# A two-layer gated encoder in one core: later stores of keys and values, gate products copied out of their banks, an earlier attention, and last tiles in halves

## The chip, the cores and the metric

The kernel runs on one core of one Trainium2 chip. The time is device time in microseconds (us). The kernel before takes 2231.48 us, the median of 3 runs (2231.09 to 2231.74). A profile and a trace of one execution stand beside it.

## The reference, cut to what matters

A trunk of 2 layers is applied to a prompt of 512 tokens and a sample of 1024 tokens, width 1024, all in float32:

```python
hn = rmsnorm(h, ln1[i]);  z = hn @ w_in[i]
q, k, v, ga, uf, gf, mga, mgf = split(z)
a = band_attention(rope(q), rope(k), v, sink[i]) * silu(ga)
f = fourier_mix(uf, w_fmix[i]) * silu(gf)
merged = sigmoid(mga) * (a @ w_ao[i]) + sigmoid(mgf) * (f @ w_fo[i])
h = h + merged @ w_out[i]
gate = sigmoid(rmsnorm(h, ln_pg[i]) @ w_pg[i])
h = h + (p[i] @ w_pe[i]) * gate
# after both layers
y = rmsnorm(h, ln_f)
```

## The kernel before, in words

**Tiles.** Tokens are cut into three chunks of 512 (`NCH`): chunk 0 is the prompt, chunks 1 and 2 the sample. Activations lie transposed, 128 channels by 512 tokens a tile. Every float32 product is made of three float32r matmuls of 512 columns (high by high, high by low, low by high; `mm3_steps`, L94), so that one output tile of 128 x 512 over 1024 channels is 24 matmuls. `hi_lo` (L84) makes the two halves: ScalarE casts (L86) and VectorE subtracts (L87).

**Stages of a layer.** `project_prompt` (L489) makes the 34 column tiles of `z` for chunk 0, in the order K, V, four of Q, then gates and U. `project_pair` (L503) makes them for chunks 1 and 2 together, two column tiles a round, by a Strassen-like scheme of 7 products (`Pair.steps`, L218) in three PSUM banks; a round has 14 steps of 6 matmuls, and its weights, 1 MB, are loaded by `Pair.load` (L192, DMAs of L195 and L196) from the third product of the round before. VectorE adds the banks up (L240 to L258). `merge` (L528) does the output projections and the gate, for chunk 0 alone (`mm_ps`, three banks of the tag mm) and then for chunks 1 and 2; in the last layer the gate of chunks 1 and 2 goes group by group, (1,) and then (2,).

**Who runs beside whom.** `run` (L938) steps a main generator (TensorE's stream of matmuls) and, from a given step on and at a given rate, a second one beside it. Beside `project_pair` runs the attention of the sample (`attention`, L668, slim: scores of a unit, loads of the next, four empty steps, values), from step 70, at 1.4 steps a step (L1036). A unit is one block of 128 queries and one key head.

**Late actions and the order of the queue.** `after(n, fn)` puts an action `n` ticks behind; `tick` runs what is due, once a step. `store` (L276) issues a DMA on SyncE's queue that way and pins it behind what stands on that queue already (`keep_in_program_order`). The queue issues in order: an issue that waits for its data holds up the loads behind it. K's stores are put 6 ticks behind, V's 3 (L440, L423). The order of everything that isn't pinned is a planner's, which sorts the instructions of each engine by program order and by when it expects their inputs. Tiles come from pools (45 tiles of 4 KB a partition under the tag act, 16 of 2 KB under scr) and are waited for when a pool is empty.

**The gate.** In `merge` the last product of a tile stays in its PSUM bank until `finish` (L580) has multiplied it (L585) by the row scale of the norm. For the first tile that scale is still to come: `norm2.stats` (L321: TensorE sums squares, L324; 12 small VectorE instructions) and `scale` (L338: four transposes, L341, and a copy, L343) come one tick behind. `finish` then does tanh on ScalarE (L586), two VectorE instructions (L587, L589), a square (L318) and its addition (L319).

**The end.** After chunk 1's and chunk 2's last tile `norm.stats` comes 1 tick and `result` (L594) 4 ticks behind: the scale, then eight tiles of the output, six by VectorE (L602) and two by ScalarE and GpSimd (L599, L600), each stored by one DMA (L603). For chunk 2 all of this comes after TensorE's last product.

Of the kernel before, what the change touches and what calls it, by code (L numbers as in the profile page):

```python
# [18 lines left out]
P = 128  # L19
# [3 lines left out]
T = 512  # L23
# [3 lines left out]
NCH = 3  # L27
EPS = 1e-6
# [11 lines left out]
def trunk(ctx: ExitStack, tc: tile.TileContext, x, p, w_in, w_af, w_out, w_pe, w_pg, w_fm,  # L40
# [53 lines left out]
    def mm3_steps(out, ws, xs, each):  # L94

        n = len(ws)
        for i, ((wh, wl), (xh, xl)) in enumerate(zip(ws, xs)):
            PE.matmul(out, wh, xh, start=i == 0, stop=False)  # L98
            PE.matmul(out, wh, xl, start=False, stop=False)  # L99
            PE.matmul(out, wl, xh, start=False, stop=i == n - 1)  # L100
            if (i + 1) % each == 0 and i + 1 < n:
                yield
# [205 lines left out]
    class Norm:  # L308
# [12 lines left out]
        def stats(self):  # L321
            st = pst("misc")
            for j in range(4):
                PE.matmul(st[:, j : j + 1], self.acc[:, j * P : (j + 1) * P], mean_sb, start=True, stop=True)  # L324

            v, y, z = (st[:, 4 * j : 4 * j + 4] for j in range(1, 4))
            r = sbt([P, 4], F32, "tiny")
            V.tensor_scalar(v, st[:, 0:4], EPS, None, op0=ALU.add)

            V.tensor_scalar(y.bitcast(I32), v.bitcast(I32), 1, None, op0=ALU.arith_shift_right)  # L330
            V.tensor_scalar(r.bitcast(I32), y.bitcast(I32), -1.0, float(0x5F3759DF), op0=ALU.mult, op1=ALU.add)
            for _ in range(3):
                V.tensor_tensor(z, v, r, op=ALU.mult)
                V.scalar_tensor_tensor(z, z, -0.5, r, op0=ALU.mult, op1=ALU.mult)
                V.scalar_tensor_tensor(r, z, 1.5, r, op0=ALU.add, op1=ALU.mult)
            self.r = r

        def scale(self):  # L338
            rb_ps, r = pst("misc"), self.r
            for j in range(4):  # L340
                PE.transpose(rb_ps[:, j * P : (j + 1) * P], r[:, j : j + 1].to_broadcast([P, P]), ident_sb)  # L341
            rb = scr()
            V.tensor_copy(rb, rb_ps)  # L343
            return rb
# [48 lines left out]
    class Projection:  # L393
# [19 lines left out]
        def transposed(self, a, c):  # L413
            s, pos = CHUNK_SEQ[c], CHUNK_POS[c]
            tp = pst("misc")
            for j in range(4):
# [7 lines left out]
                  f(t).rearrange("p j h d -> p j (h d)"), 3)  # L424

        def finish(self, m, c, out, in_sbuf):
# [9 lines left out]
            if m == MT_K:  # L436
                t = self.roped(out, c, 0)
                for r in (0, 64):
                    for kv in range(2):
                        store(K[s][r : r + 64, kv, :, pos : pos + T], f(t)[64 * kv : 64 * kv + 64], 6)  # L440
# [87 lines left out]
    def merge(l, chunks, parts, ws, bank, groups):  # L528
# [51 lines left out]
        def finish(m, c, out):  # L580
            if m == 0:
                rb[c] = norm2[c].scale()
            pl, a = scr(), scr()
# [10 lines left out]
        def result(c):  # L594
            r = norm[c].scale()
            for m in range(KD):
                o, h, g = scr(), hs[c][m // 2][:, m % 2, :], ln_sb[:, 4, m : m + 1]
                if m % 3 == 2:
                    S.activation(h, h, AF.Copy, scale=g)  # L599
                    G.tensor_tensor(o, h, r, op=ALU.mult)  # L600
                else:
                    V.scalar_tensor_tensor(o, h, g, r, op0=ALU.mult, op1=ALU.mult)  # L602
                SY.dma_start(y[c, m], o)  # L603

        for group in groups:
            for m in range(KD):
                w = ws.get()
                for c in group:
# [59 lines left out]
    def attention(l, chunks, slim):  # L668
# [91 lines left out]
        if slim:  # L760
            for u in range(len(units)):
# [3 lines left out]
                for _ in range(4):  # L765
# [243 lines left out]
    for l in range(DEPTH):  # L1009
# [21 lines left out]
        for _ in pair_made(xs, l, range(3, 4)):  # L1031
# [4 lines left out]
            (chain(attention(l, PAIR, True), mixed(0, range(8), fx)), 14 * 5, 1.4),  # L1036
# [120 lines left out]
```

## Time and profile before

| what | value |
|---|---|
| median of 3 runs | 2231.48 us |
| the profiled execution's own time | 2233.25 us |
| its span in the trace | 2231.5 us |
| TensorE busy | 2172.4 us, 97% of the span |
| VectorE, ScalarE, GpSimd busy | 1500.9, 1087.7, 297.3 us |
| TensorE's granted clock, mean | 0.991 of full speed |

A matmul's busy time is modelled and overlaps the next one's, so the list of waits (who waited for whom, and how long) says more than the busy share: TensorE's waits are where its stream broke. A wait is named by the engine and line that waited and by what came last before it went on.

### The profile page before, as it was taken

The page shows a single profiled execution, that of the slowest core. Times are in us where ns is not written, and L with a number is a line of the kernel's source. Part 1 is how long each engine was busy: PE and PEld are TensorE (multiplying, and loading weights), DVE is VectorE, ACT ScalarE, POOL GpSimd, SP SyncE. Part 2 cuts the span into 40 slices and gives each one's busy share as a digit, 9 for nine tenths or more (in the row PEclk, how much of TensorE's full clock was granted, in tenths as well). Part 3 has the DMA queues.
Part 4 walks back from the last instruction along what each step waited for, and adds up shares of the span by engine and source line. Part 5 has one row for each costly group of instructions (what it writes and reads, how often), then busy time and mean ns, then how long its engine had stood idle before and what let it go on. Part 6 is the DMA issues. An engine that isn't in the chain of part 4 may idle for free. (4 is left out here: it accounts for less than half of the span.)

```text
span 2231.5 us, 29985 instructions
## 1 busy us (share of the span) xinstructions
PE 2172.4 (97%) x10176; PEld 1803.0 (81%) x10176; DVE 1500.9 (67%) x2871; ACT 1087.7 (49%) x2324; POOL 297.3 (13%) x215
## 2 busy tenths in 40 slices
PE   9999999999999999999999999999999999999996
PEld 7778877788888878888888877778888888888885
DVE  5866576676678873464566766756766787854476
ACT  5576433566665454124324944236666644512342
POOL 0201110000002111222300010100000011231141
PEclk9999999999999999999999999999999999999998
DMA  8656454544448575532455555443444674653232
GB/s 305 221 175 210 159 173 149 159 133 153 137 153 294 190 259 190 202 104 71 144 180 170 166 171 189 160 151 128 154 152 143 208 260 170 218 203 118 78 126 99
DMA packets 241145, 380.69 MB, mean 171 GB/s; under 512 B 21216, under 2 KB 95584, under 8 KB 240992
## 3 DMA queue, kind: packets, MB, share of 16 engines
q1 hardware_dynamic: 234080, 366.19, 48.6%
q10 hardware_dynamic: 6912, 12.59, 1.5%
q8 instruction: 80, 1.31, 0.2%
q14 instruction: 73, 0.60, 0.1%
HBM read 270.17 MB, written 108.53 MB: 170 GB/s over the span
## 5 line engine op out<-in xcount | busy, mean ns | idle before, releaser
L229 PE MATMUL mm<-act,act 128*128 128x512 f32 x2856 | 694.4, 393 | 11.8 <-DVE scr L246 6.5
L229 PEld LDWEIGHTS mm<-act,act 128*128 128x128 f32 x2856 | 530.9, 188 | 124.1 <-ACT act L86 9.1
L98 PE MATMUL mm<-act,act 128*128 128x512 f32 x1384 | 545.9, 395 | 3.6 <-DVE scr L585 3.3
L100 PE MATMUL mm<-act,act 128*128 128x512 f32 x1384 | 544.2, 394 | 2.9 <-DVE act L87 2.8
L99 PE MATMUL mm<-act,act 128*128 128x512 f32 x1384 | 543.4, 393 | 0.0
L86 ACT CAST act<-act 128x512 fp32r<-128x512 f32 x574 | 329.2, 618 | 210.3 <-DMA act<-in_w_af 59.3
L87 DVE TENSOR_TENSOR act<-act,act 128x512 fp32r<-128x512 f32 x474 | 332.1, 735 | 32.4 <-ACT act L86 30.8
L100 PEld LDWEIGHTS mm<-act,act 128*128 128x128 f32 x1384 | 261.5, 189 | 59.9 <-DVE act L87 6.4
L98 PEld LDWEIGHTS mm<-act,act 128*128 128x128 f32 x1384 | 261.8, 189 | 55.7 <-issue 3.7
L99 PEld LDWEIGHTS mm<-act,act 128*128 128x128 f32 x1384 | 261.7, 189 | 52.0
L87 DVE TENSOR_TENSOR act<-scr,act 128x512 fp32r<-128x512 f32 x256 | 180.5, 727 | 56.3 <-ACT act L86 55.1
L86 ACT CAST act<-scr 128x512 fp32r<-128x512 f32 (+1 forms) x260 | 152.8, 614 | 128.8 <-DVE scr L410 65.8
L87 POOL TENSOR_TENSOR act<-act,act 128x512 fp32r<-128x512 f32 x100 | 142.5, 1450 | 324.9 <-ACT act L86 274.5
L318 ACT ACTIVATE scr<-act 128x512 f32<-128x512 f32 x105 | 65.1, 632 | 221.2 <-DVE act L569 141.7
L755 POOL TENSOR_TENSOR scr<-scr,scr 128x512 f32<-128x512 f32 x24 | 33.0, 1375 | 882.9 <-DVE scr L752 857.7
L87 DVE TENSOR_TENSOR act<-misc,act 128x512 fp32r<-128x512 f32 x132 | 88.2, 686 | 74.1 <-ACT act L86 73.8
L717 ACT ACTIVATE act<-act,stat 128x385 f32<-128x385 f32 (+1 forms) x192 | 110.6, 579 | 48.0 <-DVE stat L714 47.5
L714 DVE CUSTOM_DVE_ANT_0 act<-sc,mask_sb,nsink_sb 128x384 f32<-128x384 f32 (+1 forms) x192 | 104.4, 570 | 41.8 <-PE sc L706 41.1
L86 ACT CAST act<-misc 128x512 fp32r<-128x512 f32 x132 | 73.9, 587 | 105.9 <-PE misc L741 104.5
L98 PE MATMUL sc<-act,act 128*128 128x512 f32 (+1 forms) x308 | 118.0, 383 | 5.2 <-ACT act L86 5.2
L100 PE MATMUL sc<-act,act 128*128 128x512 f32 (+1 forms) x308 | 117.1, 380 | 0.0
L99 PE MATMUL sc<-act,act 128*128 128x512 f32 (+1 forms) x308 | 117.0, 380 | 0.0
(199 smaller groups left out, 2612.0 us busy)
## 6 DMA issues: line engine op xcount, KB each, us to landing
act<-in_w_in SPq DMA_DIRECT2D x136, 256.0 KB, 4.6
act<-in_w_in SPq DMA_DIRECT2D x68, 512.0 KB, 4.7
gt<-scr SPq DMA_DIRECT2D x96, 256.0 KB, 2.3
scr<-gt SPq DMA_DIRECT2D x96, 256.0 KB, 5.3
act<-in_w_pg SPq DMA_DIRECT2D x80, 256.0 KB, 3.9
act<-in_w_af SPq DMA_DIRECT2D x64, 256.0 KB, 5.3
act<-in_w_out SPq DMA_DIRECT2D x64, 256.0 KB, 5.1
pl<-scr ACTq DMA_DIRECT2D x48, 256.0 KB, 3.1
```

Source lines behind the costliest of these rows:

```text
L86: S.copy(hi, src)
L87: lo_eng.tensor_tensor(lo, src, f(hi), op=ALU.subtract)
L98: PE.matmul(out, wh, xh, start=i == 0, stop=False)
L99: PE.matmul(out, wh, xl, start=False, stop=False)
L100: PE.matmul(out, wl, xh, start=False, stop=i == n - 1)
L229: PE.matmul(bank, w, v, start=first and k == 0 and n == 0, stop=k == 3 and n == 2, skip_group_check=True)
L318: S.activation(sq, h, AF.Square)
L714: V.tensor_tensor_reduce(out=pr[:, :W], in0=sc[:, :W], in1=msk, scale=-0.125, scalar=nsink_sb[:, l, head : head + 1], op0=ALU.add, op1=ALU ...
L717: S.activation(pr, pr, AF.Exp, bias=nmx[:, e], scale=-1.0, accum_out=rs[:, e])
L755: G.tensor_tensor(a2, a2, gate, op=ALU.mult)
```

## The change

Five things are done, all in the functions printed above. (1) The DMAs that store K and V are put 10 ticks behind instead of 6 and 3. (2) In the gate of chunk 0 (`len(chunks) == 1`, both layers) the first two products are copied out of their banks by ScalarE, and both are finished at the third tile's tick. (3) The attention of the sample is begun 3 steps sooner, and its first unit has 8 empty steps ahead of its values instead of 4. (4) In the last layer the norm of chunk 2 for the gate is made during chunk 1's gate, and the results of chunks 0 and 1 are spread over four ticks, two tiles each. (5) The last two gate tiles of chunk 2 are done as halves of 256 tokens: first half a of both tiles, then half b; half a's statistics stand between the matmuls of b's last tile, its results beside b's end; the last square isn't added on VectorE but by a second matmul in the statistics; the row scale is read from PSUM; VectorE's and part of TensorE's instructions there are pinned in program order.

```diff
-    def mm3_steps(out, ws, xs, each):
+    def mm3_steps(out, ws, xs, each, keep=lambda i: i):
...
-            PE.matmul(out, wh, xh, start=i == 0, stop=False)
+            keep(PE.matmul(out, wh, xh, start=i == 0, stop=False))
...
+        def stats_steps(self, js, rest=None, keep=lambda i: i):
+            st, n = pst("misc"), len(js)
+            for i, j in enumerate(js):
+                PE.matmul(st[:, i : i + 1], self.acc[:, j * P : (j + 1) * P], mean_sb, start=True, stop=rest is None)
+                if rest is not None:
+                    PE.matmul(st[:, i : i + 1], rest[:, i * P : (i + 1) * P], mean_sb, start=False, stop=True)
...
+            yield keep(V.tensor_scalar(v, st[:, 0:n], EPS, None, op0=ALU.add))
...
+        def scale_ps(self, rb_ps, n=4):
+            for j in range(n):
+                PE.transpose(rb_ps[:, j * P : (j + 1) * P], self.r[:, j : j + 1].to_broadcast([P, P]), ident_sb)
...
             store(VV[s][pos // P : pos // P + 4].rearrange("j p d -> p j d"),
-                  f(t).rearrange("p j h d -> p j (h d)"), 3)
+                  f(t).rearrange("p j h d -> p j (h d)"), 10)
...
-                        store(K[s][r : r + 64, kv, :, pos : pos + T], f(t)[64 * kv : 64 * kv + 64], 6)
+                        store(K[s][r : r + 64, kv, :, pos : pos + T], f(t)[64 * kv : 64 * kv + 64], 10)
...
-        def finish(m, c, out):
-            if m == 0:
+        def finish(m, c, out, in_sbuf=False):
+            if c not in rb:
                 rb[c] = norm2[c].scale()
-            pl, a = scr(), scr()
+            pl, a = scr(), out if in_sbuf else scr()
             SY.dma_start(pl, PL[l][c][m])
             V.tensor_tensor(a, out, rb[c], op=ALU.mult)
...
         def result(c):
             r = norm[c].scale()
             for m in range(KD):
...
+                after(1 + m // 2, lambda m=m: result_tile(c, m, r))
+        def result_tile(c, m, r):
...
+        keep = tc.keep_in_program_order
+        class Half:
+            def __init__(self, c, i):
+                self.c, self.i, self.at = c, i, slice(i * HT, (i + 1) * HT)
+            def tile(self, m, out, pl):
+                c, ts = self.c, self.at
+                a, h = scr()[:, :HT], hs[c][m // 2][:, m % 2, ts]
+                yield keep(V.tensor_tensor(a, out[:, :HT], rb[c][:, ts], op=ALU.mult))
+                S.activation(a, a, AF.Tanh, scale=0.5)
+                yield keep(V.scalar_tensor_tensor(a, a, 1.0, pl[:, ts], op0=ALU.add, op1=ALU.mult))
+                yield keep(V.scalar_tensor_tensor(h, a, 0.5, h, op0=ALU.mult, op1=ALU.add))
+                self.sq = scr()[:, :HT]
+                S.activation(self.sq, h, AF.Square)
+                if m + 1 < KD:
+                    acc = norm[c].acc[:, ts]
+                    yield keep(V.tensor_tensor(acc, acc, self.sq, op=ALU.add))
+            def stats(self):
+                n = norm[self.c]
+                yield from n.stats_steps(range(2 * self.i, 2 * self.i + 2), self.sq, keep)
+                self.rb = any_ps()
+                n.scale_ps(self.rb, 2)
+            def results(self, helped):
+                c, ts = self.c, self.at
+                if helped:
+                    r = scr()[:, :HT]
+                    S.copy(r, self.rb[:, :HT])
+                for m in range(KD):
+                    if m % 2 == 0:
+                        o = scr().rearrange("p (k t) -> p k t", k=2)
+                    h, g = hs[c][m // 2][:, m % 2, ts], ln_sb[:, 4, m : m + 1]
+                    if helped and m % 4 == 3:
+                        S.activation(h, h, AF.Copy, scale=g)
+                        G.tensor_tensor(o[:, m % 2, :], h, r, op=ALU.mult)
+                    else:
+                        keep(V.scalar_tensor_tensor(o[:, m % 2, :], h, g, self.rb[:, :HT], op0=ALU.mult, op1=ALU.mult))
+                    if m % 2:
+                        SY.dma_start(y[c, m - 1 : m + 1, :, ts].rearrange("k p t -> p k t"), o)
+                    yield
+        def last_tiles(c, m0):
+            w, pl, (a, b) = {}, {}, [Half(c, i) for i in range(2)]
+            for m in range(m0, KD):
+                w[m], pl[m] = ws.get(), scr()
+                SY.dma_start(pl[m], PL[l][c][m])
+            def product(h, m, between=None):
+                out = any_ps()
+                steps = mm3_steps(out[:, :HT], w[m], [(x[:, h.at], y[:, h.at]) for x, y in parts[c]], 2, keep)
+                next(steps)
+                if between is not None:
+                    next(between)
+                for _ in steps:
+                    pass
+                return h.tile(m, out, pl[m])
+            def steps(g, n=99):
+                for _ in range(n):
+                    next(g, None)
+            for m in range(m0, KD):
+                steps(product(a, m))
+                tick()
+                yield
+            while late:
+                tick()
+            for m in range(m0, KD - 1):
+                steps(product(b, m))
+                yield
+            sa = a.stats()
+            t = product(b, KD - 1, sa)
+            steps(sa, 7)
+            steps(t, 1)
+            steps(sa)
+            steps(t)
+            ra, rb2 = a.results(False), b.stats()
+            steps(ra, NF)
+            steps(rb2)
+            steps(ra)
+            steps(b.results(True))
+            yield
         for group in groups:
-            for m in range(KD):
+            end = KD - LAST if last and group == groups[-1] and len(groups) > 1 else KD
+            for m in range(end):
                 w = ws.get()
                 for c in group:
                     out = bank()
                     yield from mm3_steps(out, w, parts[c], 4)
                     tick()
-                    if m == 0:
+                    early = len(chunks) == 1 and m < 2
+                    if early:
+                        a = scr()
+                        S.copy(a, out)
+                        out = a
+                    if m == 0 and c not in rb:
                         norm2[c].stats()
-                        after(min(2, len(group)), lambda c=c, out=out: finish(0, c, out))
+                        after(2 if early else len(group), lambda c=c, out=out, early=early: finish(0, c, out, early))
+                    elif early:
+                        after(2 - m, lambda c=c, out=out, m=m: finish(m, c, out, True))
                     else:
                         finish(m, c, out)
+                    if m == 4 and last and group != groups[-1]:
+                        n = groups[-1][0]
+                        norm2[n].stats()
+                        after(2, lambda n=n: rb.update({n: norm2[n].scale()}))
                     yield
-            if last:
+            if end < KD:
+                yield from last_tiles(group[0], end)
+            elif last:
                 for c in group:
                     after(1, norm[c].stats)
-                    after(4, lambda c=c: result(c))
+                    after(3, lambda c=c: result(c))
...
-                for _ in range(4):
+                for _ in range(4 if u else 8):
...
-            (chain(attention(l, PAIR, True), mixed(0, range(8), fx)), 14 * 5, 1.4),
+            (chain(attention(l, PAIR, True), mixed(0, range(8), fx)), 14 * 5 - 3, 1.4),
```

## Rows read from the trace of the kernel before

**Rows 1.** The page, part 1: busy us, share of the span, instructions of TensorE.

```profile
PE 2172.4 (97%) x10176; PEld 1803.0 (81%) x10176; DVE 1500.9 (67%) x2871; ACT 1087.7 (49%) x2324; POOL 297.3 (13%) x215
```

**Rows 2.** TensorE's waits, whole span: line waited for, us in all, times, longest.

```profile
PE mm L229 <- DVE scr L246: 6.5, 4, 2.5
...
PE mm L229 <- ACT act L86: 4.0, 4, 1.2
...
PE mm L98 <- DVE scr L585: 3.3, 2, 1.7
PE misc L741 <- ACT act L722: 2.9, 2, 1.5
```

**Rows 3.** Timeline of SyncE's queue, 284 to 322: start, us, line, transfer.

```profile
286.19 0.48 SPq L196 DMA_DIRECT2D act<-in_w_in  x1
308.35 0.38 SPq L277 DMA_DIRECT2D v<-act  x1
...
313.32 1.57 SPq L195 DMA_DIRECT2D act<-in_w_in  x1
```

**Rows 4.** Timelines of ScalarE, VectorE, TensorE around 320: in brackets idle before, releaser.

```profile
320.69 0.62 ACT L86 CAST act<-act 128x512 fp32r<-128x512 f32 x1 [4.72 <-issue]
...
321.34 0.69 DVE L87 TENSOR_TENSOR act<-act,act 128x512 fp32r<-128x512 f32 x1 [4.32 <-ACT act L86]
...
322.78 2.06 PE L229 MATMUL mm<-act,act 128*128 128x512 f32 x8 [2.50 <-DVE scr L246]
```

**Rows 5.** TensorE's waits from 333 to 342, and from 1421 to 1424.

```profile
PE mm L229 <- ACT act L86: 1.2, 1, 1.2
...
PE mm L229 <- DVE scr L246: 2.2, 1, 2.2
```

**Rows 6.** Timeline of TensorE, 396 to 409.

```profile
401.57 0.64 PE L706 MATMUL sc<-act,scr 128*128 128x256 f32 x4
402.05 0.86 PE L229 MATMUL mm<-act,act 128*128 128x512 f32 x3
...
404.91 1.64 PE L741 MATMUL misc<-ident_sb,act 128*128 128x128 f32 x8 [1.46 <-ACT act L722]
407.12 0.80 PE L746 MATMUL o<-act,act 128*128 128x512 f32 x1 [0.57 <-ACT act L86]
```

**Rows 7.** Stretches: busy us of each engine (instructions), granted clock, DMA share, GB/s.

```profile
407.00:410.00 3.00, 2.88 (x9) 2.49 (x10) 2.90 (x7) 3.00 (x10) 0.00 (x0) 0.52 0.00 0
...
1506.00:1510.00 4.00, 3.61 (x11) 3.08 (x12) 3.63 (x9) 4.00 (x13) 0.00 (x0) 0.57 0.02 6
...
816.00:820.00 4.00, 3.67 (x10) 2.89 (x11) 2.51 (x5) 1.89 (x3) 0.00 (x0) 0.59 0.24 91
```

**Rows 8.** Timeline of TensorE, 811 to 818 and 1911 to 1916.

```profile
814.01 0.65 PE L341 MATMUL misc<-ident_sb,tiny 128*128 128x128 f32 x4 [1.32 <-DVE tiny L335]
816.33 0.47 PE L98 MATMUL mm<-act,act 128*128 128x512 f32 x1 [1.67 <-DVE scr L585]
...
1913.81 0.47 PE L98 MATMUL mm<-act,act 128*128 128x512 f32 x1 [1.60 <-DVE scr L585]
```

**Rows 9.** Timelines of TensorE and VectorE, 2208 to the end.

```profile
2208.36 0.39 PE L100 MATMUL mm<-act,act 128*128 128x512 f32 x1
2215.25 1.84 PE L324 MATMUL misc<-mean_sb,scr 128*128 128x1 f32 x8 [6.50 <-DVE scr L319]
2219.65 1.09 PE L341 MATMUL misc<-ident_sb,tiny 128*128 128x128 f32 x4 [2.57 <-DVE tiny L335]
...
2221.51 6.17 DVE L602 SCALAR_TENSOR_TENSOR scr<-act,ln_sb,scr 128x512 f32<-128x512 f32 x6
```

**Rows 10.** Groups by line and shape: busy us, mean ns of one, idle before.

```profile
L870 DVE TENSOR_TENSOR scr<-scr,misc 128x256 f32<-128x256 f32 x40 | 16.4, 415 | 7.9 <-ACT scr L869 7.8
...
L869 ACT COPY scr<-misc 128x256 f32<-128x256 f32 x40 | 14.9, 373 | 45.6 <-PE misc L864 45.4
...
L98 PEld LDWEIGHTS mm<-act,act 128*128 128x128 f32 x1384 | 261.8, 189 | 55.7 <-issue 3.7 <-ACT act L86 0.9 <-ACT scr L460 0.5
```

More of the change, by code (lines that the diff above doesn't have):

```diff
@@ L27 @@
 NCH = 3
+HT = T // 2
+LAST = 2
+NF = 4
 EPS = 1e-6
@@ L321, in stats @@
         def stats(self):
[L322 to L331, printed above, removed]
@@ L332, in stats @@
-            for _ in range(3):
[L333 to L336, printed above, removed]
+            for _ in self.stats_steps(range(4)):
+                pass
[5 more added lines that the diff above has]
+                    PE.matmul(st[:, i : i + 1], rest[:, i * P : (i + 1) * P], mean_sb, start=False, stop=True)
+            v, y, z = (st[:, 4 * j : 4 * j + n] for j in range(1, 4))
+            self.r = r = sbt([P, n], F32, "tiny")
+            yield keep(V.tensor_scalar(v, st[:, 0:n], EPS, None, op0=ALU.add))
+            yield keep(V.tensor_scalar(y.bitcast(I32), v.bitcast(I32), 1, None, op0=ALU.arith_shift_right))
+            yield keep(V.tensor_scalar(r.bitcast(I32), y.bitcast(I32), -1.0, float(0x5F3759DF), op0=ALU.mult, op1=ALU.add))
+            for _ in range(3):
+                yield keep(V.tensor_tensor(z, v, r, op=ALU.mult))
+                yield keep(V.scalar_tensor_tensor(z, z, -0.5, r, op0=ALU.mult, op1=ALU.mult))
+                yield keep(V.scalar_tensor_tensor(r, z, 1.5, r, op0=ALU.add, op1=ALU.mult))
@@ L338, in scale @@
+        def scale_ps(self, rb_ps, n=4):
+            for j in range(n):
+                PE.transpose(rb_ps[:, j * P : (j + 1) * P], self.r[:, j : j + 1].to_broadcast([P, P]), ident_sb)
         def scale(self):
-            rb_ps, r = pst("misc"), self.r
-            for j in range(4):
-                PE.transpose(rb_ps[:, j * P : (j + 1) * P], r[:, j : j + 1].to_broadcast([P, P]), ident_sb)
+            rb_ps = pst("misc")
+            self.scale_ps(rb_ps)
             rb = scr()
@@ L596, in result @@
             for m in range(KD):
[L597 to L603, printed above, removed]
+                after(1 + m // 2, lambda m=m: result_tile(c, m, r))
+        def result_tile(c, m, r):
+            o, h, g = scr(), hs[c][m // 2][:, m % 2, :], ln_sb[:, 4, m : m + 1]
+            if m % 3 == 2:
+                S.activation(h, h, AF.Copy, scale=g)
+                G.tensor_tensor(o, h, r, op=ALU.mult)
+            else:
+                V.scalar_tensor_tensor(o, h, g, r, op0=ALU.mult, op1=ALU.mult)
+            SY.dma_start(y[c, m], o)
@@ new lines, in merge @@
+        keep = tc.keep_in_program_order
[29 more added lines that the diff above has]
+                    if helped and m % 4 == 3:
+                        S.activation(h, h, AF.Copy, scale=g)
+                        G.tensor_tensor(o[:, m % 2, :], h, r, op=ALU.mult)
+                    else:
+                        keep(V.scalar_tensor_tensor(o[:, m % 2, :], h, g, self.rb[:, :HT], op0=ALU.mult, op1=ALU.mult))
+                    if m % 2:
+                        SY.dma_start(y[c, m - 1 : m + 1, :, ts].rearrange("k p t -> p k t"), o)
+                    yield
@@ new lines, in last_tiles @@
+        def last_tiles(c, m0):
[10 more added lines that the diff above has]
+                for _ in steps:
+                    pass
+                return h.tile(m, out, pl[m])
[23 more added lines that the diff above has]
+            yield
```

## The prediction, as made before the result was known

> **What bounds the kernel now.** I read the page first: TensorE is busy for 97% of the span [rows 1], so a change that adds no matmuls to speak of can only gain where TensorE's stream is broken, and at the end, after its last product. So the list of what TensorE waited for comes next [rows 2]. It is short, and three of its entries lie in the functions that the change edits: the pair projection (L229, waiting for L246 and for weight casts of L86), the gate (L98 waiting for L585) and the attention's transposes (L741). Then I opened each place in the timelines of the engines, and the clock there, since a broken stream costs twice when the granted clock falls afterwards.
>
> *Pair projection.* SyncE issues the weights of one round at 286.19, then nothing until V's store at 308.35; the next round's weights, behind V's and K's stores, go out at 313.32 [rows 3]. ScalarE, due to cast them, stands idle for 4.72 us until 320.69, VectorE for 4.32 behind it, and TensorE, whose bank VectorE should have emptied, for 2.50 [rows 4]. Some 15 us later TensorE waits another 1.2 for a cast, and the second layer shows the first of these waits with 2.2 [rows 5]; its cast wait is the other long one of the four in [rows 2], 1.2 again.
>
> *Attention's start.* The second pair of scores of the first unit is made at 401.57, and the transposes of its probabilities, the next thing in the stream, wait 1.46 and the first product with V another 0.57 [rows 6]. The granted clock is 0.52 over the 3 us after 407, about the lower of its two levels (1.2 GHz); the second layer shows 0.57 over 4 us [rows 7].
>
> *Gate of chunk 0.* With all three banks taken, the transposes wait 1.32 for the norm's small instructions, the next matmul 1.67 for the bank that L585 empties; the clock is 0.59 over the 4 us that follow. In the second layer only the bank is late, by 1.60 [rows 7, 8].
>
> *The end.* TensorE's last product starts at 2208.36 and the span ends at 2231.5: 23.1 us of serial work, in which TensorE waits 6.50 for the last tile's chain, VectorE does the 12 small instructions between 2217.1 and 2219.65, and six results take 6.17 [rows 9].
>
> **The change part by part.**
>
> *Stores of K and V.* Nothing is added; fifteen stores a layer move behind: eight of K and two of V for the pair, four and one for the prompt's chunk. A round has 14 ticks. V's first store falls from tick 14 to 21, K's from 15 to 19, the later ones from 16 and 19 to 23, and the load of the third round stands between ticks 18 and 19: it now passes all of them. It could go out right after 286.2, as soon as its two buffers are free. The upper end is all four waits, 2.50 + 1.2 + 2.2 + 1.2 = 7.1; the lower end is 0, if the buffers come free no earlier than 313. I take 6.5, near the upper end: buffers of the round before are given back round by round, so 10 us of the 26 us of blocking is enough, since the load needs to be only 4.7 us sooner. Late next are Q's stores, which wait for casts, and the third load behind them, but those casts come 4 us sooner too. Who reads K and V (the attention) starts 60 us later, so later landing costs nothing. For the prompt the moved stores pass weight loads as well, where TensorE shows no such wait: 0.
>
> *Attention 3 steps sooner.* Three steps of 6 matmuls are 18 x 0.23 = 4.1 us (three matmuls of 512 take 0.86, the last modelled with 0.39: some 0.23 a step [rows 6, 9]). The first unit's loads and scores move by that; its values stay, since 4 more empty steps at 1.4 a step are 2.9 steps. Softmax then ends 4.1 us sooner against 1.46 + 0.57 us of waiting. With the waits goes the slow clock: 3.0 x 0.48 = 1.4 and 4 x 0.43 = 1.7 us. Both layers: 2 x (1.46 + 0.57) + 3.1 = 7.2 at most, 0 if the scores stay where they are; I take 6.7, as half a wait of L746 may stay (it occurs in later units too). The loads pass two gate stores on SyncE's queue, which have nobody waiting close behind.
>
> *Gate copies.* Four more copies of 512 columns on ScalarE, beside it. The bank is free after a copy instead of after the scale, and the transposes stand a tile (5.5 us) later, when the small instructions are long done. Gone: 1.32 + 1.67 + 4 x 0.41 + 1.60 = 6.2; I take 6.0. Three tiles are then finished at one tick: some 3 x 2.2 us of VectorE in a tile's 5.5, and the banks beyond are free meanwhile. If that cover fails, one bank wait of 1.6 comes back.
>
> *Norm of chunk 2 and results of chunk 1.* The same instructions, elsewhere; VectorE is no longer held by six results in a row just before the last tiles. That is why the next part starts with VectorE at most half a microsecond behind.
>
> *Last tiles in halves.* TensorE: 96 matmuls of 256 columns at 0.12 (four scores of 256 between 401.57 and 402.05 [rows 6]) instead of 48 at 0.23: +0.5. The statistics of half a inside b's last tile: 8 weight loads with one column, up to 1.84 as in [rows 9], 1.0 at the full clock: +1.0. After the last product, by 256-column prices of 0.415 for VectorE and 0.373 for ScalarE [rows 10]: scale, tanh, two products, square 2.0, handovers 0.3, VectorE behind 0.5: 2.8. Statistics 1.1; the 12 small instructions 2.4, behind what is left of a's first four results (4 x 0.415, partly beside the statistics) 0.8; two transposes 0.6, with a's other four results beside and behind them 1.7 in all; b's six results 6 x 0.415 = 2.5; the last store and the closing 3.3 (before: from 2227.7 to 2231.5, 3.8, behind a queue of stores). Together 2.8 + 1.1 + 2.4 + 0.8 + 1.7 + 2.5 + 3.3 = 14.6, and 0.4 for the last product itself. So 23.1 - 15.0 - 1.5 = 6.6; I take 6.5, between 2 (VectorE's pinned order makes b's statistics late and a's statistics hold TensorE up) and 8. Six results beside GpSimd's two took 1.03 each at twice the columns [rows 9], by which six halves would be 3.1 instead of 2.5; the sum goes by the row of one operand in PSUM. The Trainium skill, "SBUF — State Buffer", section "Who interferes with whom", says that a VectorE instruction contends with GpSimd's reads only if both its inputs are in SBUF, and the change puts the scale in PSUM; by that the 2.5 stands, and the six results of 1.03 before agree with the contention.
>
> *The planner.* A moved instruction makes it sort everything anew. Small waits come with any order: of L246's four, 6.5 in all [rows 2], two are under a microsecond. I charge 2.7, three such, between a gain of 1 and a loss of 9.
>
> **Sum.** 6.5 + 6.7 + 6.0 + 6.5 - 2.7 = 23.0. The profiled execution took 2233.25 (span 2231.5 and 1.75 around it), so 2210.25 there; the median of the runs is 1.8 below it: 2208.5.
>
> **The rivals.**
>
> *The load waits for buffers, not for the queue* (0.13). The pool of 45 may have none free until the round is over. For it: nothing in the trace says when they are free. Against: the load before went out 27 us earlier, a whole round and more. Then 2208.5 + 6.5 = 2215.
>
> *The halves pay for their weights* (0.10). Each half needs the same weights loaded again. A load is busy for 0.189 [rows 10]; if that set the step, 96 x 0.189 - 96 x 0.12 = 6.6 more: 2215. Against it stand the scores, 0.12 a step with weights of their own. The Trainium skill, "TensorE: Matmul & The Clock Gate", section "The mechanism", says that a weight load overlaps running matmuls only when the row group differs; by that, at its figure of 107 ns for 128 columns, 48 loads more would cost 5.1. The trace disagrees: 512 columns at 0.23 and 256 at 0.12 leave no room for it.
>
> *The first scores don't move* (0.05), since the planner sorts them by their inputs: the attention's 6.7 is lost, 2215.
>
> *New waits as long as the old* (0.06): two or three stalls with the clock's fall, each 3.5 like the attention's: 2219, and with the first rival 2225.
>
> *Slower* (0.04): the tiles of K and V are kept up to 7 steps, 9.7 us, longer from the pool of 45. If the weight loads are what runs dry, each of four projections starts its rounds up to 9.7 late: 39 - 25.7 gives 2245. It decides from 6.4 us a projection; the first stores went out at 308 and later before as well [rows 3], about where tick 19 stands, so the tiles are hardly kept longer than they were.
>
> **How the numbers follow.** My forecast has 0.62. All terms at their upper ends and no charge give 2231.5 - 28.5 = 2203, and the modelled ends of matmuls hide 0.1 to 0.2 more in each wait: 2200 is the low end. 2219 takes in the rivals at 2215 and half of the fourth. About 0.2% (4.5 us) is what a measurement of this kernel can tell from no change: only the fifth rival is slower, 0.04, and the fourth's worst with the tail's lower end lies within, 0.04. Faster: 0.92.
>
> **What would show it.** Right: no idle time of ScalarE near 316 to 320, the third round's weights issued before 308 and before V's store; no wait of L741 after the first scores and the clock at 1.00 there; no wait for L585 after chunk 0's first gate tiles; 256-column matmuls at 0.12 a step; 14 to 16 us from the last product to the end. Wrong: a weight load that waits although the queue is free, L746 or L741 waits of 1.5 as before, or a new entry in TensorE's list over 2 us.

## The result, and the profile after

Compared on one chip, the changed kernel takes 2211.47 us (median of 4 runs, 2208.93 to 2213.0), the kernel before 2231.61: a ratio of 0.9904, 95% interval 0.989 to 0.9917. It is 20.1 us faster; the forecast was 2208.5, a gain of 23.0, with a range of 2200 to 2219. The profiled execution took 2211.66 (span 2209.9; mean granted clock 0.995, before 0.991). In the code after, the helpers' lines stand 3 further down, the pair projection's L229 and L246 are L232 and L249, the attention's L706, L741 and L746 are L828, L863 and L868, the gate's L585 is L598, the norm's L324 and L341 are L333 and L350.

Page after, part 1, which answers to [rows 1]:

```profile
PE 2165.4 (98%) x10232; PEld 1802.1 (82%) x10232; DVE 1503.5 (68%) x2896; ACT 1090.2 (49%) x2333; POOL 296.7 (13%) x215
```

TensorE's waits over the span after (line waited for: us in all, times, longest), to be laid beside [rows 2]:

```profile
PE o L868 <- ACT act L89: 4.0, 4, 1.5
PE mm L103 <- DVE act L90: 3.7, 5, 1.0
PE mm L232 <- ACT act L89: 3.6, 4, 1.1
PE mm L350 <- DVE tiny L346: 2.5, 1, 2.5
PE misc L350 <- DVE tiny L346: 1.8, 1, 1.8
PE mm L101 <- ACT act L89: 1.8, 1, 1.8
PE mm L232 <- DVE scr L249: 1.8, 2, 0.9
PE mm L101 <- ACT scr L473: 1.7, 3, 0.7
...
PE mm L101 <- ACT scr L785: 1.6, 1, 1.6
...
PE mm L101 <- DVE scr L598: 0.5, 1, 0.5
```

Three of the four old entries are gone or small: L249 fell from 6.5 in four waits to 1.8 in two, L863 has no entry, L598 fell from 3.3 to 0.5. The fourth, the casts' 4.0, is 3.6: it stayed. What is new is L785 (1.6), L350 for L346 in the stream (1.8, at 2143.19) and L101 for a cast of L89 in the prompt's projection (1.8).

SyncE's queue in the first layer's pair projection, against [rows 3]:

```profile
286.25 0.37 SPq L198 DMA_DIRECT2D act<-in_w_in  x1
...
303.49 0.33 SPq L198 DMA_DIRECT2D act<-in_w_in  x1
...
307.09 3.10 SPq L280 DMA_DIRECT2D k<-act  x4
310.29 2.60 SPq L280 DMA_DIRECT2D v<-act  x2
```

The third round's weights go out 9.8 us sooner, now ahead of the stores that they stood behind.

Stretches after (where the attention starts; at chunk 0's gate; in the prompt's projection; in the second layer's), against [rows 7]:

```profile
407.00:410.00 3.00, 3.00 (x15) 2.49 (x14) 2.36 (x6) 2.22 (x5) 0.00 (x0) 1.00 0.71 260
816.00:820.00 4.00, 3.59 (x17) 2.66 (x16) 3.23 (x5) 1.62 (x3) 1.30 (x1) 1.00 0.35 131
...
97.00:103.00 6.00, 4.67 (x12) 3.48 (x13) 5.28 (x10) 3.28 (x7) 0.00 (x0) 0.72 0.84 263
1310.00:1316.00 6.00, 5.30 (x16) 4.51 (x17) 4.00 (x21) 2.13 (x8) 1.28 (x2) 0.57 0.23 84
```

The granted clock is 1.00 where it was 0.52 and 0.59. The one at 1310 has its like in the kernel before (0.54 over 1318 to 1324). In the prompt's projection one such stretch moved: before, it stood at 79 to 83 (0.57), behind a wait of 1.13 at 76.86; now 97 to 103 has 0.72 where it had 1.00, behind two waits:

```profile
97.44 0.50 PE L101 MATMUL mm<-act,act 128*128 128x512 f32 x1 [1.77 <-ACT act L89]
99.06 0.80 PE L103 MATMUL mm<-act,act 128*128 128x512 f32 x1 [0.90 <-DVE act L90]
```

The end, timelines of TensorE and VectorE, against [rows 9]:

```profile
2194.93 0.28 PE L102 MATMUL mm<-act,act 128*128 128x256 f32 x1
2195.05 0.28 PE L103 MATMUL mm<-act,act 128*128 128x256 f32 x1
...
2198.13 0.47 PE L335 MATMUL misc<-mean_sb,scr 128*128 128x1 f32 x2 [0.81 <-ACT scr L638]
...
2201.91 0.69 PE L350 MATMUL mm<-ident_sb,tiny 128*128 128x128 f32 x2 [2.45 <-DVE tiny L346]
...
2203.33 2.43 DVE L662 SCALAR_TENSOR_TENSOR scr<-act,ln_sb,mm 128x256 f32<-128x256 f32 x6
```

The last product starts at 2195.05, 14.85 us before the end; it was 23.1.

### The profile page after: what moved, and what is told of

Same layout as the page of the kernel before. It is cut to its first block, busy times and chain, and to the rows that moved or that the text cites. A ratio compares the mean times of both kernels' runs of the same rounds, so it can differ in the third digit from the quotient of the medians.

```text
span 2209.9 us, 30119 instructions
## 1 busy us (share of the span) xinstructions
PE 2165.4 (98%) x10232; PEld 1802.1 (82%) x10232; DVE 1503.5 (68%) x2896; ACT 1090.2 (49%) x2333; POOL 296.7 (13%) x215
## 5 line engine op out<-in xcount | busy, mean ns | idle before, releaser
L232 PE MATMUL mm<-act,act 128*128 128x512 f32 x2856 | 693.6, 393 | 6.7 <-ACT act L89 3.6
L232 PEld LDWEIGHTS mm<-act,act 128*128 128x128 f32 x2856 | 530.1, 188 | 117.2 <-ACT act L89 7.3
L101 PE MATMUL mm<-act,act 128*128 128x512 f32 (+1 forms) x1392 | 546.8, 393 | 6.1 <-ACT act L89 1.8
L103 PE MATMUL mm<-act,act 128*128 128x512 f32 (+1 forms) x1392 | 545.2, 392 | 3.8 <-DVE act L90 3.7
L102 PE MATMUL mm<-act,act 128*128 128x512 f32 (+1 forms) x1392 | 544.1, 391 | 0.0
L89 ACT CAST act<-act 128x512 fp32r<-128x512 f32 x574 | 329.7, 619 | 197.1 <-DMA act<-in_w_af 59.2
L90 DVE TENSOR_TENSOR act<-act,act 128x512 fp32r<-128x512 f32 x474 | 332.6, 736 | 24.7 <-ACT act L89 23.2
L101 PEld LDWEIGHTS mm<-act,act 128*128 128x128 f32 x1392 | 263.1, 189 | 59.2 <-ACT act L89 2.8
L89 ACT CAST act<-scr 128x512 fp32r<-128x512 f32 (+1 forms) x260 | 152.9, 615 | 130.5 <-DVE scr L423 69.5
L90 DVE TENSOR_TENSOR act<-scr,act 128x512 fp32r<-128x512 f32 x256 | 179.1, 720 | 56.0 <-ACT act L89 54.8
L90 POOL TENSOR_TENSOR act<-act,act 128x512 fp32r<-128x512 f32 x100 | 142.4, 1450 | 324.2 <-ACT act L89 312.8
L90 DVE TENSOR_TENSOR act<-misc,act 128x512 fp32r<-128x512 f32 x132 | 88.1, 685 | 72.1 <-ACT act L89 71.8
L89 ACT CAST act<-misc 128x512 fp32r<-128x512 f32 x132 | 73.8, 587 | 122.3 <-PE misc L863 120.6
L101 PE MATMUL sc<-act,act 128*128 128x512 f32 (+1 forms) x316 | 119.1, 377 | 5.8 <-ACT act L89 5.8
```

The lines of the kernel that those rows point to most:

```text
L89: S.copy(hi, src)
L90: lo_eng.tensor_tensor(lo, src, f(hi), op=ALU.subtract)
L101: keep(PE.matmul(out, wh, xh, start=i == 0, stop=False))
L232: PE.matmul(bank, w, v, start=first and k == 0 and n == 0, stop=k == 3 and n == 2, skip_group_check=True)
```

## The experiments

The forecast had three rivals at 2215 or so and a price of 0 on part 4. The first four runs undo one part each; the next ones ask why these four differences do not add up to the gain; the last look for what gave part of it back. All ratios are against the kernel before on the same chip; it takes 2230.78 to 2232.88 us on the chips used, so medians of different runs are compared less closely than ratios.

**K's and V's stores back at 6 and 3 ticks.**

```diff
-store(VV[s]..., 10)
+store(VV[s]..., 3)
-store(K[s]..., 10)
+store(K[s]..., 6)
```

> The changed kernel with K's and V's stores back at 6 and 3 ticks. Theory (the queue held the third round's weights up): TensorE's wait for VectorE's bank addition at the start of the pair projection is back in both layers, 2.2 to 2.5 us each, the load goes out behind V's store, and the kernel is about 5 us slower than the changed one. Rival (the load waits for its buffers, and the wait went away because the new order of VectorE's work suits better): the waits stay away, and the time is within 2 us of the changed kernel's.

2213.9 us, ratio 0.9915 (0.99 to 0.993). TensorE's waits, and SyncE's queue:

```profile
PE mm L232 <- DVE scr L249: 6.0, 4, 2.4
```

```profile
308.50 0.38 SPq L280 DMA_DIRECT2D v<-act  x1
...
313.47 1.57 SPq L198 DMA_DIRECT2D act<-in_w_in  x1
```

The old waits are back with the old order of the queue, and the weights again go out behind V's store, so it was the queue that held them. The time is only 2.4 us above the changed kernel's 2211.47, some half of what these waits cost, and the two intervals overlap.

**Attention as before.**

```diff
-for _ in range(4 if u else 8):
+for _ in range(4):
-14 * 5 - 3, 1.4
+14 * 5, 1.4
```

> The changed kernel with the attention begun at step 70 again and 4 empty steps. Theory (first softmax late, the clock falls behind it): waits of the first transposes of 1.4 to 1.5 us and of the first product with V of 0.6 us are back in both layers, the granted clock falls to about 0.5 for 3 us behind them, 8 to 9 us slower than the changed kernel. Rival (prediction's price, waits with half of the clock's loss): 6 to 7 us. Rival (other units take the waits over): under 3 us.

2216.4 us, ratio 0.9932 (0.9909 to 0.9955), some 5 us above the changed kernel. TensorE's waits, and two stretches:

```profile
PE misc L863 <- ACT act L844: 2.9, 2, 1.5
```

```profile
407.00:410.00 3.00, 2.44 (x9) 2.00 (x10) 2.07 (x5) 2.69 (x7) 0.00 (x0) 0.56 0.00 0
1503.00:1506.00 3.00, 3.00 (x10) 2.43 (x10) 3.00 (x9) 3.00 (x11) 0.00 (x0) 0.50 0.02 5
```

This is the entry of [rows 2], and the clock is near its lower level again. Its four runs lie between 2212.3 and 2224.5 (the profiled one), so the time decides between none of the three expectations; the waits and the clock speak for the first two.

**Gate products not copied.**

```diff
-early = len(chunks) == 1 and m < 2
+early = False
```

> The changed kernel without the copies of the first gate products. Theory (6.9 us of waits and slow clock taken out at the first gate tiles, some 4 us given back 30 us later where the next layer's embedding starts and waits for banks): waits of 1.3 to 1.7 us at L598 and L350 are back, those at the embedding's start (1.6 us for L785) are gone, and the kernel is 2 to 4 us slower than the changed one. Rival (the waits at the embedding have nothing to do with the gate): 6 to 7 us slower, with the waits for L785 still there.

2211.46 us, ratio 0.9904 (0.9888 to 0.9921): no difference from the changed kernel in the median, though the intervals leave room for some 4 us, and though the waits are back. TensorE between 805 and 855 waits in two places, and in no other, and its clock is 0.50 over 810 to 815:

```profile
807.88 0.65 PE L350 MATMUL misc<-ident_sb,tiny 128*128 128x128 f32 x4 [1.28 <-DVE tiny L346]
810.20 0.76 PE L101 MATMUL mm<-act,act 128*128 128x512 f32 x1 [1.67 <-DVE scr L598]
```

With the copies, these two waits are gone and others stand behind: 0.41 and 0.40 at 818 and 824, and some 35 us later 0.54 at 846.49 and 1.59 at 849.74, for L785. Laid side by side by the starts of the same VectorE and ScalarE instructions, the changed kernel's trace gains 2.1 on this run's at the gate of the first layer and 1.9 at the second's, and loses 2.6 near 1310, where it waits 1.74 for a cast against 0.60 here and its clock is low for longer. So the copies' 6.0 is worth some 4 in this pair of traces, part of it is given back within the stage, and what is left is lost in the scatter.

**Last tiles whole.**

```diff
-end = KD - LAST if last and group == groups[-1] and len(groups) > 1 else KD
+end = KD
```

> The changed kernel with the last two gate tiles of chunk 2 whole again; results of chunk 1 still spread, norm of chunk 2 still early. Theory (the halves shorten the serial end from some 21 to 14.9 us and cost TensorE 1.5 us): 4 to 6 us slower than the changed kernel, since the spread results alone take the 2 us by which VectorE was behind. Rival (the end is shorter because VectorE was freed of the burst of results, not by the halves): within 2 us of the changed kernel.

2214.64 us, ratio 0.9918 (0.9903 to 0.9933), 3.2 above: between the two expectations, with intervals that overlap. Its end, timelines of TensorE and VectorE:

```profile
2189.39 0.39 PE L103 MATMUL mm<-act,act 128*128 128x512 f32 x1
2194.16 1.83 PE L333 MATMUL misc<-mean_sb,scr 128*128 128x1 f32 x8 [4.38 <-DVE scr L322]
...
2200.48 6.11 DVE L619 SCALAR_TENSOR_TENSOR scr<-act,ln_sb,scr 128x512 f32<-128x512 f32 x6
```

Span 2210.4, so 21.0 from the last product to the end: of the 8.3 that the end lost, the halves make 6.2 and the spread results, which stand here too, 2.1 (the wait of 6.50 in [rows 9] is 4.38).

The four differences make 2.4 + 5 + 0 + 3.2 = 10.6 of 20.1. Two runs asked where the rest is.

**Parts 1 to 3 undone together** (the edits of the first three runs in one kernel).

> The changed kernel with its first three parts undone together (stores 3 and 6 steps behind, attention's start as before, no copies of gate products); the tail's halves, the earlier norm of chunk 2 and the spread results stay. Theory A, the parts add up as undoing one at a time showed them (stores 2.4, attention 5, copies 0): 2211.5 + 7.4 = 2219. Theory B, the prediction's terms hold and undoing one part at a time understates them, because the order is planned anew and the waits of the others shift: 6.5 + 6.7 + 6.0 - 2.7 = 16.5 is lost, about 2228, or, if the tail with the norm and the spread keeps its 6.5, 2225. Both: TensorE waits again for L249 (about 6.5 in all), for the attention's L844 and for the gate's L598, and the clock is near 0.5 to 0.6 after 407 and 1506.

2226.31 us (11 runs), ratio 0.9981 (0.9971 to 0.999). Theory B's time: together the three parts are worth about 15 us by the medians (17 by the ratios). That undoing one alone understates this is not shown. Theory A's 7.4 was added up from medians of four runs each, which scatter by up to 12 us; by the profiled spans the three single runs stand 1.8, 12.8 and 0.8 above the changed kernel, 15.4 together, and this one 12.6. TensorE's waits are the old ones; the clock is low after 1500 (0.57 over 1500 to 1508), but 1.00 over 407 to 410, behind the same waits of 1.4 and 0.6 that it fell after in the kernel before:

```profile
PE mm L232 <- DVE scr L249: 5.5, 4, 2.1
...
PE mm L101 <- DVE scr L598: 3.3, 2, 1.7
...
PE misc L863 <- ACT act L844: 2.9, 2, 1.5
```

**K's and V's stores alone, in the kernel before** (both at 10, nothing else).

> The kernel before with the stores of K and V 10 steps behind and nothing else changed. Theory A, the part is worth what its four waits and no more cost (6.5 in the prediction, 5 if the casts' 1.2 at 335 and 1435 stays): 5 to 6.5 us faster, L246's two waits over 2 us gone. Theory B, undoing it in the changed kernel gave its worth (2.4): 2 to 3 us faster, with new waits in the projections' place.

2227.55 us (12 runs) against 2232.88, ratio 0.9978 (0.9968 to 0.9988): 5.3 us. The waits over 2 us are gone, as by Theory A; of Theory B's 2 to 3 us the interval leaves out 2.4, but not 3, so Theory A is the likelier and not settled. Here, too, L246 keeps two waits of 1.8 in all, and the casts' 3.6 stay.

**Part 4 undone** (the norm of chunk 2 where it was; results of chunk 1 in one burst).

```diff
-if m == 4 and last and group != groups[-1]:
+if False:
-after(1 + m // 2, lambda m=m: result_tile(c, m, r))
+result_tile(c, m, r)
-after(3, lambda c=c: result(c))
+after(4, lambda c=c: result(c))
```

> The changed kernel with the norm of chunk 2 made where it was before and the results of chunk 1 in one burst, as before. Theory A, these two are worth nothing by themselves (the prediction's price): 2210.5 to 2212.5. Theory B, the new wait of 1.8 us at 2143 (the transposes of chunk 2's scale, for the small instructions of the norm) is the early norm's price, and without it TensorE doesn't wait there: 2209.5, if nothing takes its place at chunk 2's first gate tiles. Theory C, the part of the gain that undoing single parts did not find (20.1 - 10.6 = 9.5 us) lies here: about 2217 to 2221, with VectorE behind at the last tiles, and over 17 us from the last product to the end.

2217.41 us, ratio 0.994 (0.9926 to 0.9954): 6 us above the changed kernel by the medians, 8 by the ratios. Theory C's size, with its wait ahead of the last product instead of behind it. VectorE's timeline, TensorE's waits, and two stretches:

```profile
2172.02 7.17 DVE L619 SCALAR_TENSOR_TENSOR scr<-act,ln_sb,scr 128x512 f32<-128x512 f32 x6
```

```profile
PE misc L333 <- DVE scr L641: 4.5, 1, 4.5
```

```profile
2190.00:2195.00 5.00, 1.24 (x6) 1.18 (x6) 3.16 (x8) 1.88 (x5) 0.00 (x0) 0.50 0.00 0
2195.00:2200.00 5.00, 5.00 (x24) 4.94 (x24) 2.30 (x12) 0.42 (x1) 0.00 (x0) 0.50 0.00 0
```

The burst makes VectorE late for the first half: its first scale starts at 2189.43 instead of 2186.80, although TensorE starts that half at 2178.22 instead of 2182.49, so it is 6.9 us further behind, about the burst's 7.17. Half a's statistics stand inside b's last tile, so TensorE waits 4.5 there for the addition of a square (L641) and 1.5 for the last square, with products still to do, and then makes them at half the clock: 24 instructions in 5 us. Whether the halves without part 4 lose more than they bring would take a run with parts 1 to 3 alone, and there is none.

**The second layer's input projections with banks of all three pools**, since L785 holds a bank of the gate's pool.

```diff
-out = any_ps() if l == 0 else pst("mm")
+out = any_ps()
```

> The changed kernel with one edit: the projections of the second layer's input (L782) take their banks from all three pools, not from the pool that the gate of chunk 0 uses too. Theory A, the copies of the gate did gain, but it was given back because this work waited for a bank of that pool (0.54 at 846.5 and 1.59 at 849.7, some 4 us of steps lost between 815 and 850): no wait for L785 or L598 there, 2207.5 to 2209.5. Theory B, what was lost there is late vector work and late loads, whatever the bank: the wait moves to another bank or to a load, 2210.5 to 2212.5.

2215.54 us, ratio 0.9938 (0.9918 to 0.9957): slower than the changed kernel. Theory B's mechanism, and a longer time than it gave; the wait moves from L785 to the gate:

```profile
PE mm L101 <- DVE scr L598: 5.8, 2, 3.6
```

As the trace reads, the projections, no longer held, run ahead, and the gate's next tile then finds its bank not yet scaled by VectorE.

**The same, with the norm of chunk 2 a tile sooner and its scale two more ticks behind.**

```diff
-if m == 4 and last and group != groups[-1]:
+if m == 3 and last and group != groups[-1]:
-after(2, lambda n=n: rb.update(...))
+after(4, lambda n=n: rb.update(...))
```

> As the run before, and also the norm of chunk 2 started one tile sooner, its scale made two more tiles behind (4 instead of 2). Theory A, the wait of 1.8 us at 2143 is for VectorE's small instructions, which stand between other work in the order: it goes, and the time is 1.5 to 2 below the run before, 2206 to 2208. Theory B, the wait moves to another place of the same tiles: the same time as the run before, within 1.

2215.15 us, ratio 0.9925 (0.9911 to 0.994). The wait of 1.8 at 2143 is gone from the list, the time is that of the run before. Whether it was given back or is lost in the scatter of the runs (2211.5 to 2215.7) stays open.

**The changed kernel again**, as the reference of the two runs that follow.

> The changed kernel unaltered, on the chip of the next three runs, as their reference: 20 us faster than the kernel before, as in the first comparison (0.9904, 0.989 to 0.9917). If its ratio comes out near 0.993 instead, then the last call's four ratios are to be read against that, and neither the norm nor the spread is worth what it seemed there.

2211.13 us (2207.62 to 2212.33), ratio 0.9899 (0.9886 to 0.9912): as the first time. In its trace the two waits of the prompt's projection stand again, 1.77 at 97.12 and 0.90 at 98.75, but the clock does not fall behind them:

```profile
97.00:103.00 6.00, 4.98 (x21) 3.82 (x22) 5.28 (x9) 3.29 (x8) 0.00 (x0) 1.00 0.94 309
```

It falls at 2142 instead, where it stood at 1.00 the first time. So the same kernel with the same waits keeps its clock in one execution and loses it in another, and differences of a few us between single traces can be this alone.

**Chunk 0's stores of h further behind.**

```diff
-store(H[c][m], h, 2)
+store(H[c][m], h, 7 if len(chunks) == 1 else 2)
```

> The changed kernel with one edit: for chunk 0 the stores of the first layer's result h stand 7 steps behind their tiles instead of 2. Theory A, the copies of the gate gave their gain back because SyncE, which issues in order, still stands at these stores until h is made (808 to 815.75, then before 825.5 and 841.3), with the last weights and the pl loads of the gate's last tiles behind them: the weights that went out at 820.8 go out before 812, the pl loads of 841.7 before 838, VectorE's 1.75 at 844.42 and TensorE's waits for L598 (0.54) and L785 (1.59) go, and it is 2 to 4.5 us faster than the unaltered one. Theory B, the weights wait for free tiles of the pool, not for the queue: their issue stays at 820 to 840, same time.

2207.7 us (2205.53 to 2210.51), ratio 0.9888 (0.9875 to 0.9901): 3.4 below the run before by the medians, 2.5 by the ratios, the fastest kernel of this study, though the intervals overlap. SyncE's queue in the kernel after:

```profile
815.75 4.96 SPq L280 DMA_DIRECT2D h<-act  x3
820.80 1.83 SPq L157 DMA_DIRECT2D act<-in_w_af  x4
...
841.30 0.33 SPq L280 DMA_DIRECT2D h<-act  x1
841.72 0.88 SPq L597 DMA_DIRECT2D scr<-pl  x2
```

and in this one:

```profile
812.09 6.71 SPq L157 DMA_DIRECT2D act<-in_w_af  x4
...
837.51 0.90 SPq L597 DMA_DIRECT2D scr<-pl  x2
```

The weights go out from 812.09 and the last loads of pl (the tile of `p[i] @ w_pe` that the gate multiplies) 4.2 us sooner, and the waits of 835 to 850 are gone: first the stretch after, then here (the second figure is TensorE's busy time):

```profile
835.00:850.00 15.00, 12.88 (x56) 10.05 (x55) 11.59 (x15) 6.59 (x12) 3.05 (x2) 1.00 0.22 80
```

```profile
835.00:850.00 15.00, 15.00 (x68) 12.12 (x67) 12.09 (x16) 7.90 (x15) 3.14 (x2) 1.00 0.30 104
```

Theory A. The trace shows the waits gone, and by the starts of the same VectorE and ScalarE instructions the stage takes 2.5 us less than in the run before; that the whole kernel gains by it is likely rather than settled.

**The edit on banks and the one on h together.**

> As the run before, with the banks of the second layer's input projections taken from all three pools too. Theory A of the run before: with vector work and loads in time the bank matters little, and it is within 1 us of the run before. Rival: the bank of the gate's pool is what the projections wait for, and only here do the waits at 845 to 850 go: 2 us or more below the run before.

2212.47 us, ratio 0.9911 (0.9898 to 0.9923), above the run with h alone: neither expectation. TensorE waits for L598 again (3.8 in two waits, 3.1 the longest), although the loads are in time, so it seems that the bank that held the projections back was what kept VectorE's work for the gate in step.

## Why the prediction was right, point by point

**The sum.** By the profiled spans the gain is 2231.5 - 2209.9 = 21.6 where 23.0 was forecast. The terms, read off the two traces: stores 5.1 (6.5 - 1.8 for VectorE, 4.0 - 3.6 for casts), attention 7.2, copies 6.2, the end 23.1 - 14.85 - 1.5 = 6.75, together 25.2 with the 1.5 of the forecast for TensorE's added work; the 3.6 down to 21.6 went to new waits. What each place was worth net is read from the starts of the same VectorE instruction in the two traces:

| instruction, line before and after | before | after | ahead | since the row above |
|---|---|---|---|---|
| first layer's pair, L246, L249 | 298.01 | 298.51 | -0.5 | prompt -0.5 |
| the same, later | 362.75 | 360.33 | 2.4 | stores 2.9 |
| chunk 0's merge, L546, L559 | 691.74 | 685.10 | 6.6 | attention 4.2 |
| next chunks' merge, L544, L557 | 890.49 | 882.78 | 7.7 | copies 1.1 |
| second layer's pair, L246, L249 | 1397.54 | 1389.67 | 7.9 | 0.2 |
| the same, later | 1462.01 | 1451.50 | 10.5 | stores 2.6 |
| chunk 0's merge, L544, L557 | 1790.17 | 1775.47 | 14.7 | attention 4.2 |
| chunk 1's norm for its gate, L328, L339 | 2123.06 | 2106.51 | 16.6 | copies 1.9 |
| end of the span | 2231.5 | 2209.9 | 21.6 | the end 5.0 |

So the stores brought 5.5 (5.0 with what the prompt lost) where 6.5 was forecast, the attention 8.4 for 6.7, the copies 2.9 for 6.0, and the end 5.0 for 6.5, the new wait at 2143 included. The sum fits as well as it does because the attention's surplus and the charge of 2.7 make up for terms that were too large: the total's closeness is partly luck. Each trace is one execution, so a few us between places are the clock's. The other 1.6 of the 3.0 by which 2208.5 was too low is the execution that was profiled: before, it lay 1.8 above the median, and I carried that over; after, it lies 0.2 above.

**Stores, 6.5.** The mechanism is right, the term mis-sized. The two waits for VectorE went (2.50 and 2.2); the two for casts stayed, 1.06 at 335.48 instead of 1.2. The step that failed is the sum "2.50 + 1.2 + 2.2 + 1.2", which put the casts' waits down to the queue too: ScalarE casts the rotated tile first, for whose sum on VectorE (L423) it stands idle 4.69 us until 334.29, and the weights behind it, whenever they were loaded. For the same sum it stands idle 8.76 until 325.78, so the sign "no idle time of ScalarE near 316 to 320" did not come, though TensorE waits for nothing there. The load, which "could go out right after 286.2" if its buffers were free, went at 303.49, with nothing of its queue ahead of it: SyncE waited 7.8 us for VectorE's L90 and then 8.5 for TensorE's L232, the readers of earlier weights. That is the first rival's mechanism, 10 us too early to hurt. The prompt's price of 0 was nearly right, but not because nothing happened: the waits of 97 to 99 stand in every run with the moved stores, in the kernel before with them alone too, and not in the two runs with K's and V's stores put back; in exchange the wait of 1.13 at 76.86 shrinks to 0.60 at 76.73, and 0.5 is lost in all.

**Attention, 6.7.** Right, a little more than forecast. The first scores started at 386.6 instead of 396.3, 9.7 us sooner rather than 4.1; 2.4 of it is the lead that the stream had there, and why the rest, 7.3, is more than the three steps' 4.1 stays open. Nothing of the waits stayed, so 7.2 by waits and clock, and 8.4 by the table. The third rival fell.

**Copies, 6.0.** Right at the place (6.2 gone), half as much for the kernel: 2.9 by the table, some 4 against the run that undid them, and nothing that the medians can tell. The step that failed is "the banks beyond are free meanwhile", which looked at one tile. SyncE's queue stands from 808.5 to 815.75 at a store of h, with weights and pl loads behind it; TensorE, which no longer loses 1.32, 1.67 and the clock's 1.6 there, reaches what that queue feeds too soon. With the stores of h moved, the waits of 835 to 850 went. I had looked for such queueing at K and V and not here, where the same helper with 2 ticks does the same thing.

**The end, 6.5.** Right: 14.85 instead of 15.0, with two sizes inside that were off and cancel. The statistics of b start 3.08 after the last product (forecast 3.2), take 1.1, the scale comes at 2201.91, b's six results take 2.43 (forecast 2.5), and the closing is 2209.9 - 2205.76 = 4.1 instead of 3.3; against that, the 0.8 for a's first four results is gone, as they end at 2199.20, before the small instructions start at 2199.49. The second rival fell: 256 columns with weights of their own step at 0.12 (2194.93 to 2195.05). The rule of the Trainium skill, "TensorE: Matmul & The Clock Gate", section "The mechanism", by which such loads would not overlap, is again not borne out. The six results took 0.405 each beside GpSimd's two with the scale in PSUM, and 1.02 each at twice the columns with both inputs in SBUF, where the halves were undone. Without GpSimd the halves of a took 0.41 each, and whole tiles at 2188.56, two in 1.41, 0.70. That agrees with the Trainium skill, "SBUF — State Buffer", section "Who interferes with whom".

**Part 4, priced at 0.** By itself that may hold, and it was named as what keeps VectorE in time; but its absence costs 6 to 8, by a wait inside the stream and the clock's fall, and its early norm waits 1.81 at 2143. The term belonged beside the end's: cover of a pinned order has a price.

**The planner, 2.7.** 3.6 by the spans. The new waits are those named above: 1.77 and 0.90 in the prompt, 0.41, 0.40, 0.54 and 1.59 at the gate, 1.81 at 2143, less old ones that went. They are not all the planner's, though: the prompt's come with the moved stores, the gate's with SyncE's queue. The fourth rival (stalls as long as the old) came half true: the one at 97 to 103 had the clock's fall with it in one execution and not in another. The slower case did not come: TensorE's list has no new wait over 2 us ahead of its last product.

## What to carry to other kernels

Where loads and stores share a queue that issues in order, look at every store that waits for data not yet made, and move it behind the loads of the next tiles; after one such place is mended, the next one sets the pace. Price an edit that keeps another in time by what the other loses without it, not by its own instructions. Undoing one part of a change tells what it is worth among the others, and only as far as the runs agree: three parts came to 7.4 one by one and to some 15 together by medians, where four runs of one kernel lay up to 12 us apart, and to 15.4 and 12.6 by the profiled spans. Laying two traces side by side by the starts of the same instructions showed where the time went when the medians could not.

## What was not expected of the hardware

The runs of one kernel scatter with the granted clock: the stores alone in the kernel before took 2223.61 to 2233.59 us, at mean clocks of 0.993 and 0.989. Apart from the tail, the clock stood at the lower level, 1.2 GHz, for 20.5 us of the span before and 10.2 of the span after, worked out from the granted clock along the two spans, so that about 5 of the 21.6 us came back through the clock; each such stretch followed an idle time of TensorE of some 1 to 3 us (as at 97 to 99), but not every idle time was followed by one (846 to 850 was not, and 97 to 99 was in one execution of the changed kernel and not in the other).
